# A recurrent layer's block pipeline: projections in another order, scores by pairs of heads, short products inside units, one staged transposition

## The chip, the cores and the metric

The kernel runs on one core of a Trainium2 chip. The number that counts is the device time of one execution in microseconds (us). The core's engines work side by side, each through its own list of instructions in the order of that list: TensorE (PE; its weight loads are shown as PEld), VectorE (DVE), ScalarE (ACT), GpSimd (POOL) and SyncE (SP), which issues the DMA transfers. An instruction that waits for another engine holds up all that stand behind it in its list. Sums of products build up in PSUM, everything else lies in SBUF, in 128 partitions.

## The reference

For 4096 tokens of width 1024: a normalised and modulated input `h`, one input projection, two branches, one output projection, a residual and a final norm. The part that the change touches is the second branch, RWKV-7 with 8 heads of 64 values:

```python
r, w_lo, k, v, a_lo, z = jnp.split(seg, split_idx, axis=-1)    # after a shift by one token
w_raw = -jax.nn.softplus(-(w0 + jnp.tanh(w_lo) @ w_up)) - 0.5
decay = jnp.exp(-jnp.exp(w_raw))
a  = jax.nn.sigmoid(a0 + a_lo @ a_up)
kk = k * k_k / jnp.maximum(norm(k * k_k), L2_EPS)               # per head
k  = k * (1.0 + (a - 1.0) * k_a)
# per token and head, S is 64 x 64:
S = S * w_t + (S @ -kk_t)[..., None] * (kk_t * a_t) + v_t[..., None] * k_t
y = S @ r_t
y = (group_norm(y) * ln_w + ln_b + sum(r * k * r_k) * v) * silu(z)
```

## The kernel before

Phase 1 (to 397 us) makes `h` and the pooling branch. Phase 2 takes the tokens in 16 blocks of 256, each of 4 chunks of 64. The tail (from 1820 us) is the output projection. The change lies in phase 2.

Inside a chunk the recurrence is written with matrices. For each block the kernel goes through these stages:

- `front` (L525 to L646): 17 projections of the block's tokens, called segs: `lo` (0), and for each of four pairs of heads `p` keys `kS` (1+4p), receptances `rS` (2+4p), values `vS` (3+4p) and gates `zS` (4+4p). A seg is 8 units of three 128x257 matmuls in half precision (L552 to L554); then ScalarE (L556) and VectorE (L557) evict it. After `rS` of a pair follow its short products and the decay: `pl`, `pa` (L583, L584), `tw`, `ta` (L586 to L589), a scan `L` on VectorE (L591), its exponentials `Ppad`, `Pi` (L593, L595), and the scaled operands `AR` and `BK` (L605 to L609), `rk` (L614). `cent` (L621) makes the centred values `vps` of a pair and copies them into `UV`, for the last pair also the squared norms of the keys; `late` (L635) makes the bonus `bon`.
- `scores` (L648): for each chunk eight heads' products `BK` x `AR` on TensorE, masked by VectorE into `sc` (L666).
- `inverse` (L690): the 32 diagonal 32x32 blocks of each half are transposed by VectorE into `Ab` (L703), scaled (L704) and copied (L705, L707). Then 30 pairs of VectorE steps (`Wt` L721, `W` L726) eliminate them, each pair needing the one before. The results go back through transpositions (L739, L740) to the products `qp` (L750) and `m21p` (L758) of TensorE.
- `chain` (L789): the loop over the four chunks with the state `S`. In each: `px` (L809), copies `xa` on ScalarE (L816), `psn` (L821), copies `UV` on ScalarE (L829), `psn` and `px` again (L837, L848), copies `y` (L855). After every second chunk `gn` normalises: `ysq`, `var`, `rstd` on POOL (L870), `y` (L872), and then `ytp`, `mx` (L884 to L888).

While block b goes through `scores`, `inverse` and `chain`, the units of `front` of block b+1 are put between its products by `fill(n)`: n units each, the counts in `FS` to `FY` and `FI`. `unpin` and `keep_in_program_order` fix the order of some matmuls; beyond that the framework's scheduler orders each engine's list by priority, where `high_priority(offset=PRI)` lifts the elimination, `xa` and `UV` over the next block's front. PSUM tiles come from small pools: three buffers for `pj`, which segs, `pl`, `pa`, `vps` and `pb` share, two each for `sc` and `px`, one for `psn`. A buffer is free for TensorE only when its eviction is over.

Of the kernel before, what the change touches and what calls it, by code (L numbers as in the profile page):

```python
# [52 lines left out]
def kernel(  # L53
# [426 lines left out]
    with ExitStack() as ph:  # L480
# [56 lines left out]
        def front(b, f):  # L537
# [8 lines left out]

            def seg(m, name, bufs=2):
                pp = ps_pj.tile([P, TB2 + 1], F32, tag="pj", name=f"pj{b}_{m}")
                for k in range(KT):
                    if k:  # L550
                        yield
                    unpin(PE.matmul(pp, w2_hi[m][:, k, :], hh[k], start=(k == 0), stop=False))  # L552
                    PE.matmul(pp, w2_hi[m][:, k, :], hl[k], start=False, stop=False)  # L553
                    PE.matmul(pp, w2_lo[m][:, k, :], hh[k], start=False, stop=(k == KT - 1))  # L554
                sg = wk.tile([P, TB2], F32, tag=name, name=f"{name}{b}_{m}", bufs=bufs)
                A.activation(sg, pp[:, 1:], AF.Identity, bias=0.0, scale=c1[:, m : m + 1])  # L556
                V.scalar_tensor_tensor(sg, pp[:, :TB2], c2[:, m : m + 1], sg, op0=ALU.mult, op1=ALU.add)  # L557
                return sg
# [12 lines left out]
            todo = []  # L571
            sqs = []
            for p in range(NPAIR):
                kS = yield from seg(1 + 4 * p, "kS")
                sq = wk.tile([P, TB2], F32, tag=f"sq{p}", name=f"sq{b}_{p}")
                sqs.append(sq)
                A.activation(sq, kS, AF.Square, scale=vec[:, V_KK + p : V_KK + p + 1])
                yield
                rS = yield from seg(2 + 4 * p, "rS")
# [16 lines left out]
                if todo:  # L596
                    todo.pop(0)()
                yield
                vS = yield from seg(3 + 4 * p, "vS")
                if p == 0:  # L600
                    BK = f["BK"] = blk.tile([P, NPAIR, NCH, 2, C], F32, tag="BK", name=f"BK{b}")
# [5 lines left out]
                V.tensor_mul(ta, ta, kS)  # L607
                V.tensor_mul(AR[:, p, :, 1, :], c3(rS), Pp[:, :, 1:])
                V.tensor_mul(BK[:, p, :, 1, :], c3(ta), c3(Pi))  # L609
                G.tensor_copy(pc[:, p, :], Pp[:, :, C])  # L610
                if todo:
                    todo.pop(0)()
                rk = wk.tile([P, TB2], F32, tag="rk", name=f"rk{b}_{p}")
                V.scalar_tensor_tensor(rk, rS, pv[:, HRK, p : p + 1], ta, op0=ALU.mult, op1=ALU.mult)  # L614
                yield
                zS = yield from seg(4 + 4 * p, "zS")
                tz = wk.tile([P, TB2], F32, tag="L", name=f"tz{b}_{p}")
                A.activation(tz, zS, AF.Tanh, bias=0.0, scale=0.5)
                V.scalar_tensor_tensor(szt[:, p, :], tz, 1.0, zS, op0=ALU.add, op1=ALU.mult)

                def cent(p=p, vS=vS):  # L621
                    vps = ps_pj.tile([P, 4, P], F32, tag="pj", name=f"vps{b}_{p}")
                    for j in range(2):
                        PE.matmul(vps[:, j, :], vS[:, j * P : (j + 1) * P], cmat, start=True, stop=True)
                    if p == NPAIR - 1:
                        for q in range(NPAIR):
                            PE.matmul(vps[32 * q : 32 * q + 32, 2:4, :], hsel, sqs[q].rearrange("q (j t) -> q j t", j=2), start=True, stop=True)
                        A.copy(ssb.rearrange("q (j t) -> q j t", j=2), vps[:, 2:4, :])
                    for j in range(2):
                        A.copy(  # L630
                            UV[64:128].rearrange("q (c j) e -> q c j e", j=2)[:, :, j, p * P : (p + 1) * P],
                            vps[64 * j : 64 * j + 64, 0:2],
                        )

                def late(p=p, rk=rk, vS=vS):  # L635
                    pb = ps_pj.tile([P, TB2], F32, tag="pj", name=f"pb{b}_{p}")
                    PE.matmul(pb, bones, rk, start=True, stop=True)
                    V.tensor_mul(bon[:, p, :], pb, vS)  # L638

                todo = [cent, late]  # L640
                if p < NPAIR - 1:
                    yield
            f["todo"] = todo
            yield

        def scores(b, f, fill):  # L646
# [271 lines left out]
        def project(b):  # L918
# [128 lines left out]
```

## Time and profile before

| | |
|---|---|
| median of 3 runs | 2123.24 us (2123.21 to 2123.97) |
| the profiled execution | 2123.65 us, span 2121.9 us |
| mean granted clock of TensorE | 0.982 of full speed |
| PE busy | 1984.5 us (94%) |
| DVE busy | 1449.5 us (68%) |
| ACT busy | 965.5 us (46%) |
| POOL busy | 131.6 us (6%) |

Busy shares are means over phases with different limits: phase 1 and the tail are near full on TensorE alone. Matmuls overlap, so that one of them shows 0.27 us while the next begins 0.11 us later; the distance of starts is the price then. An operation on DVE or ACT overlaps its neighbour by somewhat under 0.1 us.

### The profile page before, as it was taken

To read this page: it belongs to the slowest core of one execution; us is meant where nothing else is said; L and a number is where in the kernel's file an instruction comes from. 1 tells how busy PE (TensorE), PEld (TensorE's weight loads), DVE (VectorE), ACT (ScalarE), POOL (GpSimd) and SP (SyncE) were. 2 spreads that over 40 slices of the span, in tenths; PEclk is the share of its full clock that TensorE was granted. 3 is DMA by queue.
4 is the path that set the end of the run, shared out by engine and by line. 5 is a ranking of instruction groups with operands and counts; after the bars stand their busy time and mean duration, and the time that the engine had idled before them with its cause. 6 is when DMAs were issued, how large, how long until landed. Compare 5 with 4: busy or idle time off the path is not lost.

```text
span 2121.9 us, 48336 instructions
## 1 busy us (share of the span) xinstructions
PE 1984.5 (94%) x20186; PEld 1463.6 (69%) x20186; DVE 1449.5 (68%) x3549; ACT 965.5 (46%) x2119; POOL 131.6 (6%) x262
## 2 busy tenths in 40 slices
PE   5999999999999999999999999999999989999998
PEld 2444444677777777777777777777777767788886
DVE  7898987566857768578577686786776866533333
ACT  3545433345455554554555545545555453312111
POOL 0000000000000000000000100000000000100000
PEclk8999999999999999999999999999999999999999
DMA  8867767200110110101101101011011434443431
GB/s 304 278 224 239 243 217 269 66 21 2 31 27 7 31 26 7 32 2 31 27 7 31 27 6 32 2 31 27 6 32 27 134 111 140 157 142 130 153 105 70
DMA packets 140445, 183.19 MB, mean 86 GB/s; under 512 B 12098, under 2 KB 94018, under 8 KB 140227
## 3 DMA queue, kind: packets, MB, share of 16 engines
q1 hardware_dynamic: 140226, 180.11, 26.0%
q8 instruction: 158, 2.59, 0.5%
q14 instruction: 61, 0.49, 0.1%
HBM read 121.22 MB, written 58.85 MB: 85 GB/s over the span
## 4 chain that ended last, share of the span: by engine, by line
PE 54%; DVE 28%; ACT 11%; issue 4%; DMA 2%; POOL 0%; SPq 0%; DVEq 0%; ACTq 0%; POOLq 0%
PE po L947 6%; PE po L949 5%; PE po L948 5%; PE pj L552 5%; PE pj L554 4%; PE pj L553 4%; DVE W L726 4%; DVE Wt L721 4%; PE pp L412 4%; PE pp L411 4%; PE pp L410 4%; DVE Ab L703 3%; PE psn L821 2%; PE scp_sc L659 2%; PE px L809 2%
## 5 line engine op out<-in xcount | busy, mean ns | idle before, releaser
L552 PE MATMUL pj<-hh,w2h 128*128 128x257 f16 x2176 | 609.5, 280 | 48.2 <-DVE bon L638 24.0
L554 PE MATMUL pj<-hh,w2l 128*128 128x257 f16 x2176 | 604.1, 278 | 0.0
L553 PE MATMUL pj<-hl,w2h 128*128 128x257 f16 x2176 | 602.3, 277 | 0.0
L553 PEld LDWEIGHTS <-w2h 128*128 128x128 f16 x2176 | 217.5, 100 | 87.4 <-issue 57.4
L552 PEld LDWEIGHTS <-w2h 128*128 128x128 f16 x2176 | 214.9, 99 | 52.2 <-issue 6.5
L554 PEld LDWEIGHTS <-w2l 128*128 128x128 f16 x2176 | 213.5, 98 | 34.1
L947 PE MATMUL po<-wo,mh 128*128 128x512 f32 x512 | 204.3, 399 | 3.7 <-ACT mh L931 3.7
L948 PE MATMUL po<-wo,mh 128*128 128x512 f32 x512 | 201.8, 394 | 0.0
L411 PE MATMUL pp<-lo,w1h 128*128 128x512 f16 x512 | 194.0, 379 | 1.4 <-DVE lo L225 1.4
L410 PE MATMUL pp<-hi,w1h 128*128 128x512 f16 x512 | 194.1, 380 | 1.1 <-ACT hi L224 1.1
L412 PE MATMUL pp<-hi,w1l 128*128 128x512 f16 x512 | 194.0, 379 | 0.0
L951 DVE TENSOR_TENSOR x<-po,x 128x512 f32<-128x512 f32 x64 | 44.2, 690 | 151.9 <-PE po L949 151.9
L953 ACT ACTIVATE sq<-x 128x512 f32<-128x512 f32 x64 | 40.4, 631 | 208.8 <-DVE x L951 190.6
L721 DVE TENSOR_TENSOR Wt<-W,Ab 128x30 f32<-128x30 f32 (+7 forms) x480 | 117.5, 245 | 10.2
L726 DVE TENSOR_TENSOR W<-W,Wt 128x30 f32<-128x30 f32 (+7 forms) x480 | 117.5, 245 | 9.1
L947 PEld LDWEIGHTS po<-wo,mh 128*128 128x128 f32 x512 | 96.7, 189 | 25.9 <-ACT mh L931 3.9
L948 PEld LDWEIGHTS po<-wo,mh 128*128 128x128 f32 x512 | 96.6, 189 | 22.3
L949 PE MATMUL po<-wo,ml 128*128 128x512 f32 x256 | 101.4, 397 | 0.0
L557 DVE SCALAR_TENSOR_TENSOR kS<-pj,c,kS 128x256 f32<-128x256 f32 x64 | 30.6, 478 | 100.2 <-ACT kS L556 100.2
L412 PEld LDWEIGHTS <-w1l 128*128 128x128 f16 x512 | 50.1, 98 | 61.6 <-issue 2.0
L411 PEld LDWEIGHTS <-w1h 128*128 128x128 f16 x512 | 50.1, 98 | 59.4 <-issue 1.2
L410 PEld LDWEIGHTS <-w1h 128*128 128x128 f16 x512 | 50.2, 98 | 59.0 <-issue 0.8
(243 smaller groups left out, 3814.0 us busy)
## 6 DMA issues: line engine op xcount, KB each, us to landing
x<-in_x_dram SPq DMA_DIRECT2D x64, 256.0 KB, 3.0
out_dram<-x SPq DMA_DIRECT2D x64, 256.0 KB, 2.1
xk<-in_xT_dram SPq DMA_DIRECT2D x56, 256.0 KB, 4.1
xt<-in_x_dram SPq DMA_DIRECT2D x28, 512.0 KB, 5.7
wada<-in_w_ada_dram SPq DMA_DIRECT2D x24, 512.0 KB, 5.7
w2raw<-in_w_in_dram SPq DMA_DIRECT2D x17, 512.0 KB, 5.4
hh<-hT_hi SPq DMA_DIRECT2D x32, 257.0 KB, 3.6
hl<-hT_lo SPq DMA_DIRECT2D x32, 257.0 KB, 3.0
```

Source lines behind the costliest of these rows:

```text
L410: PE.matmul(pp, w1_hi[m][:, k, :], hi, start=(k == 0), stop=False)
L411: PE.matmul(pp, w1_hi[m][:, k, :], lo, start=False, stop=False)
L412: PE.matmul(pp, w1_lo[m][:, k, :], hi, start=False, stop=(k == KT - 1))
L552: unpin(PE.matmul(pp, w2_hi[m][:, k, :], hh[k], start=(k == 0), stop=False))
L553: PE.matmul(pp, w2_hi[m][:, k, :], hl[k], start=False, stop=False)
L554: PE.matmul(pp, w2_lo[m][:, k, :], hh[k], start=False, stop=(k == KT - 1))
L703: V.transpose(Ab[o : o + 32], sc[o : o + 32, :, o : o + 32].rearrange("s i t -> s t i"))
L721: V.tensor_mul(tmp[:, :n, :k], W[:, r0:, k : k + 1].to_broadcast([P, n, k]), Ab[:, k : k + 1, :k].to_broadcast([P, n, k]),)
L726: V.tensor_add(W[:, r0:, :k], W[:, r0:, :k], tmp[:, :n, :k])
L947: unpin(PE.matmul(po, mh[:, k, ts_], wo[0][k][n], start=(k == 0), stop=False))
L948: PE.matmul(po, mh[:, k, ts_], wo[1][k][n], start=False, stop=False)
L949: PE.matmul(po, (ml[:, k] if b % 2 == 0 else ml[k])[:, ts_], wo[0][k][n], start=False, stop=(k == KT - 1))
```

## The change

Five edits in `front`, `scores` and `inverse`. The segs come in another order: `lo`, the four `zS`, the four `vS`, and then `kS` and `rS` of each pair. The short products wait in a list `pend` and are issued inside a later seg, ahead of its units 3 and 6, in place of between segs. They are `cent` (now two products only), `heavy` (the decay and the operands of a pair) and `bonus`. The keys' norms become a function of their own, `norms`, whose products have 256 columns and a PSUM tile of their own. `scores` goes by pairs of heads, all four chunks at a time, in place of by chunks with all heads. After each pair's masks ScalarE copies the diagonal blocks into the free half of `UV` (`stg`), in the order that lets `inverse` use one transposition of 64 partitions in place of two of 32. `vS` gets four buffers, `tz` its own tag.

```diff
+            pend = []
             def seg(m, name, bufs=2):
...
+                    if k in (3, 6) and pend:
+                        pend.pop(0)()
...
             for p in range(NPAIR):
-                kS = yield from seg(1 + 4 * p, "kS")
...
+                zS = yield from seg(4 + 4 * p, "zS")
+                tz = wk.tile([P, TB2], F32, tag="tz", name=f"tz{b}_{p}")
+                A.activation(tz, zS, AF.Tanh, bias=0.0, scale=0.5)
+                V.scalar_tensor_tensor(szt[:, p, :], tz, 1.0, zS, op0=ALU.add, op1=ALU.mult)
                 yield
-                rS = yield from seg(2 + 4 * p, "rS")
+
+            def cent(p, vS):
+                vps = ps_pj.tile([P, 2, P], F32, tag="pj", name=f"vps{b}_{p}")
+                for j in range(2):
+                    PE.matmul(vps[:, j, :], vS[:, j * P : (j + 1) * P], cmat, start=True, stop=True)
...
+            for p in range(NPAIR):
+                vS = yield from seg(3 + 4 * p, "vS", bufs=NPAIR)
+                vs.append(vS)
+                pend.append(lambda p=p, vS=vS: cent(p, vS))
+                yield
...
+            def heavy(p, kS, rS):
...
+            def bonus(p):
+                pb = ps_pj.tile([P, TB2], F32, tag="pj", name=f"pb{b}_{p}")
+                PE.matmul(pb, bones, rks[p], start=True, stop=True)
+                V.tensor_mul(bon[:, p, :], pb, vs[p])
...
+            def norms():
+                pn = ps_pj.tile([P, TB2], F32, tag="pj", name=f"pn{b}")
+                for q in range(NPAIR):
+                    PE.matmul(pn[32 * q : 32 * q + 32, :], hsel, sqs[q], start=True, stop=True)
+                A.copy(ssb, pn)
+
+            for p in range(NPAIR):
+                kS = yield from seg(1 + 4 * p, "kS")
...
+                if p:
+                    pend.append(lambda p=p - 1: bonus(p))
                 yield
...
+                rS = yield from seg(2 + 4 * p, "rS")
+                pend.append(lambda p=p, kS=kS, rS=rS: heavy(p, kS, rS))
                 if p < NPAIR - 1:
                     yield
-            f["todo"] = todo
+            while pend:
+                pend.pop(0)()
+            f["todo"] = [norms, lambda: bonus(NPAIR - 1)]
...
-            for ch in range(NCH):
...
+            stg = f["stg"] = f["UV"][0:64].rearrange("q c e -> q (c e)")[:, 0:1024].rearrange("q (t i) -> q t i", t=32)
+            for p in range(NPAIR):
...
+                for kb in range(2):
+                    o = 32 * kb
+                    A.copy(
+                        stg[o : o + 32].rearrange("q t (c g h) -> q t c g h", c=NCH, h=2)[:, :, :, p],
+                        sc[o : o + 32, :, o : o + 32].rearrange("q (c g h) t -> q t c g h", c=NCH, h=2)[:, :, :, p],
                     )
...
-                for kb in range(2):
-                    o = 32 * kb
-                    V.transpose(Ab[o : o + 32], sc[o : o + 32, :, o : o + 32].rearrange("s i t -> s t i"))
+                V.transpose(Ab[0:64], f["stg"])
```

Three places show how the lists move. In the names, the number behind a seg is its own (`vS_3` is the values of pair 0), `_0` to `_3` behind the others is the pair or the chunk, and `Wt_30` is the first elimination step; line numbers of the changed kernel are its own. The first place is VectorE between the last masks and the first step. Before:

```order
L666 TENSOR_TENSOR sc_12765<-scp_3_px,mask 128x4x128
L557 SCALAR_TENSOR_TENSOR kS_1_12915<-pj_1_12844,c_103,kS_1_12915 128x256
L703 STREAM_TRANSPOSE Ab_12936<-sc_12765 32x1024 x2
L638 TENSOR_TENSOR bon_11578<-pb_3_12927,vS_15_12654 128x256
L704 TENSOR_TENSOR Ab_12936<-Ab_12936,d2T_12764 64x1024
L557 SCALAR_TENSOR_TENSOR rS_2_12956<-pj_2_12920,c_103,rS_2_12956 128x256
L707 COPY W_12937<-Ab_12936 64x512 x2
L591 SCALAR_TENSOR_TENSOR L_0_12968<-rst,tw_0_12963 128x256
L721 TENSOR_TENSOR Wt_30_13037<-W_12937,Ab_12936 128x30
L726 TENSOR_TENSOR W_12937<-W_12937,Wt_30_13037 128x30
```
Now:

```order
L687 TENSOR_TENSOR sc_12826<-scp_3_sc,mask 128x4x128
L687 TENSOR_TENSOR sc_12826<-scp_3_px,mask 128x4x128
L562 SCALAR_TENSOR_TENSOR zS_4_12983<-pj_4_12921,c_103,zS_4_12983 128x256
L728 STREAM_TRANSPOSE Ab_13002<-UV_11636 64x1024
L582 SCALAR_TENSOR_TENSOR szt_12852<-tz_0_12986,zS_4_12983 128x256
L729 TENSOR_TENSOR Ab_13002<-Ab_13002,d2T_12825 64x1024
L562 SCALAR_TENSOR_TENSOR zS_8_13021<-pj_8_12989,c_103,zS_8_13021 128x256
L732 COPY W_13003<-Ab_13002 64x512 x2
L746 TENSOR_TENSOR Wt_30_13082<-W_13003,Ab_13002 128x30
L751 TENSOR_TENSOR W_13003<-W_13003,Wt_30_13082 128x30
```
One transposition stands in place of two; `bon`, `rS_2` and the scan `L_0` have left the stretch, and `zS_4`, `zS_8` and a product `szt` of the gates stand there.

The second place is VectorE where the values of pair 0 are evicted (L557 before, L562 now), on which `vps` of TensorE waits. Before, inside the fourth pair of steps:

```order
L726 TENSOR_TENSOR W_12937<-W_12937,Wt_28_13056 128x2x28
L608 TENSOR_TENSOR AR_12787<-rS_2_12956,Ppad_3664 128x4x64
L721 TENSOR_TENSOR Wt_27_13077<-W_12937,Ab_12936 128x2x27
L557 SCALAR_TENSOR_TENSOR vS_3_13022<-pj_3_12979,c_103,vS_3_13022 128x256
L726 TENSOR_TENSOR W_12937<-W_12937,Wt_27_13077 128x2x27
L607 TENSOR_TENSOR ta_0_12965<-ta_0_12965,kS_1_12915 128x256
```
Now, between the 14th pair and the 15th:

```order
L751 TENSOR_TENSOR W_13003<-W_13003,Wt_18_13210 128x7x18
L746 TENSOR_TENSOR Wt_17_13231<-W_13003,Ab_13002 128x7x17
L751 TENSOR_TENSOR W_13003<-W_13003,Wt_17_13231 128x7x17
L562 SCALAR_TENSOR_TENSOR vS_3_13159<-pj_3_13128,c_103,vS_3_13159 128x256
L746 TENSOR_TENSOR Wt_16_13234<-W_13003,Ab_13002 128x8x16
L751 TENSOR_TENSOR W_13003<-W_13003,Wt_16_13234 128x8x16
```
The eviction of `vS_3` has moved behind the step `Wt_17`, and the front's products around it are gone.

The third place is ScalarE in the third chunk (chunk 2) of the chunk loop. Before:

```order
L855 COPY y_0_13567<-px_0_13469 64x4x64
L855 COPY y_0_13567<-px_1_13470 64x4x64
L865 ACTIVATE ysq_0_13755<-y_0_13567 128x512
L604 ACTIVATE ta_3_13720<-ta_3_13720,pv 128x256
L816 COPY xa_2_13787<-px_0_13469 64x256
L816 COPY xa_2_13787<-px_1_13470 64x256
L829 COPY UV_11581<-psn_2_13769 64x4x64 x2
L855 COPY y_2_13770<-px_0_13469 64x4x64
```
Now (`UV` from `psn_2` is the copy for which TensorE waits):

```order
L880 COPY y_0_13614<-px_1_13492 64x4x64
L890 ACTIVATE ysq_0_13786<-y_0_13614 128x512
L841 COPY xa_2_13818<-px_0_13491 64x256
L841 COPY xa_2_13818<-px_1_13492 64x256
L611 ACTIVATE tw_2_13828<-pl_2_13824,pv 128x256
L613 ACTIVATE ta_2_13830<-pa_2_13825,pv 128x256
L614 ACTIVATE tw_2_13828<-tw_2_13828,one 128x256
L618 ACTIVATE Ppad_3664<-L_2_13833 128x4x64
L620 ACTIVATE Pi_2_13836<-L_2_13833 128x256
L854 COPY UV_11636<-psn_2_13800 64x4x64 x2
L626 ACTIVATE ta_2_13830<-ta_2_13830,pv 128x256
```
The copies `UV` from `psn_2` came right behind `xa_2`; now `tw`, `ta`, `Ppad` and `Pi` of pair 2 stand between.

## Rows read from the trace of the kernel before

**Rows 1.** Windows of block 7: length, busy us of PE, PEld, DVE, ACT, POOL, clock, DMA, GB/s

```profile
1045.60:1068.60 23.00, 21.29 (x203) 16.98 (x202) 17.88 (x32) 10.89 (x24) 1.88 (x3) 1.00 0.19 50
1068.60:1092.90 24.30, 22.56 (x184) 18.57 (x181) 22.31 (x85) 9.90 (x23) 0.86 (x4) 0.93 0.01 1
1102.10:1130.40 28.30, 26.69 (x605) 20.56 (x602) 12.71 (x38) 18.34 (x48) 1.93 (x2) 1.00 0.07 19
1045.60:1130.40 84.80, 78.83 (x1062) 62.57 (x1060) 61.38 (x169) 45.02 (x107) 6.05 (x11) 0.98 0.08 20
```

**Rows 2.** Waits of PE in block 7: us in total, times, longest

```profile
PE pj L552 <- DVE bon L638: 1.7, 1, 1.7
PE vps L624 <- ACT tw L586: 1.7, 3, 0.6
PE pj L552 <- DVE rS L557: 1.2, 1, 1.2
```

**Rows 3.** Timeline of DVE, block 7, masks to elimination: start, us, instruction

```profile
1060.35 0.68 DVE L666 TENSOR_TENSOR sc<-scp_px,mask 128x512 f32<-128x512 f32 x1
1061.34 3.87 DVE L703 STREAM_TRANSPOSE Ab<-sc 32x1024 f32<-32x1024 f32 x2
1067.99 0.69 DVE L591 TENSOR_TENSOR_SCAN L<-rst,tw 128x256 f32<-128x256 f32 x1
1068.60 0.16 DVE L721 TENSOR_TENSOR Wt<-W,Ab 128x30 f32<-128x30 f32 x1
```

**Rows 4.** Groups by line, whole span: busy us, mean ns of one, idle before

```profile
L740 DVE STREAM_TRANSPOSE MQ<-UV 32x1024 f32<-32x1024 f32 x16 | 19.6, 1223 | 0.8 <-ACT sq L953 0.8
L752 ACT COPY MQ<-qp 32x256 f32<-32x256 f32 x64 | 23.3, 364 | 1.6
L721 DVE TENSOR_TENSOR Wt<-W,Ab 128x30 f32<-128x30 f32 (+7 forms) x480 | 117.5, 245 | 10.2
```

**Rows 5.** Timeline of PE, block 7, around vps; idle before in brackets

```profile
1078.64 0.71 PE L624 MATMUL vps<-cmat,vS 128*128 128x128 f32 x4 [0.57 <-ACT tw L586]
1080.52 0.37 PE L552 MATMUL pj<-hh,w2h 128*128 128x257 f16 x1 [1.17 <-DVE rS L557]
1080.91 0.42 PE L554 MATMUL pj<-hh,w2l 128*128 128x257 f16 x1
1081.12 0.42 PE L552 MATMUL pj<-hh,w2h 128*128 128x257 f16 x1
```

**Rows 6.** Timeline of PE, block 7, chunk 0

```profile
1109.14 0.27 PE L553 MATMUL pj<-hl,w2h 128*128 128x257 f16 x1
1109.25 0.27 PE L554 MATMUL pj<-hh,w2l 128*128 128x257 f16 x1
1109.65 0.69 PE L837 MATMUL psn<-UV,BT 128*64 128x64 f32 x16
```

**Rows 7.** Timeline of ACT, block 7, chunk loop

```profile
1105.72 1.51 ACT L760 COPY UV<-m21p 32x256 f32<-32x256 f32 x4 [0.80 <-PE m21p L758]
1108.86 0.75 ACT L829 COPY UV<-psn 64x256 f32<-64x256 f32 x2 [0.84 <-PE psn L821]
1115.85 0.47 ACT L586 ACTIVATE tw<-pl,pv 128x256 f32<-128x256 f32 x1 [0.15 <-PE pa L584]
1116.58 0.51 ACT L589 ACTIVATE tw<-tw,one 128x256 f32<-128x256 f32 x1
1117.89 0.42 ACT L593 ACTIVATE Ppad<-L 128x256 f32<-128x256 f32 x1
1118.22 0.40 ACT L595 ACTIVATE Pi<-L 128x256 f32<-128x256 f32 x1
```

**Rows 8.** Group of the power on POOL, whole span

```profile
L870 POOL TENSOR_TENSOR rstd<-var,nhalf 128x8 f32<-128x8 f32 x32 | 54.0, 1687 | 218.9 <-DVE var L868 218.9
```

**Rows 9.** Windows of the first front and of block 4

```profile
397.60:451.30 53.70, 52.08 (x450) 44.24 (x449) 27.39 (x61) 23.60 (x54) 0.75 (x4) 1.00 0.02 7
790.30:874.40 84.10, 77.57 (x1062) 61.93 (x1061) 61.40 (x168) 44.94 (x108) 6.06 (x11) 1.00 0.08 20
```

More of the change, by code (lines that the diff above doesn't have):

```diff
@@ L570, in front @@
             c3 = lambda t_: t_.rearrange("q (c t) -> q c t", c=NCH)
-            todo = []
-            sqs = []
             for p in range(NPAIR):
-                kS = yield from seg(1 + 4 * p, "kS")
-                sq = wk.tile([P, TB2], F32, tag=f"sq{p}", name=f"sq{b}_{p}")
-                sqs.append(sq)
-                A.activation(sq, kS, AF.Square, scale=vec[:, V_KK + p : V_KK + p + 1])
+                zS = yield from seg(4 + 4 * p, "zS")
+                tz = wk.tile([P, TB2], F32, tag="tz", name=f"tz{b}_{p}")
+                A.activation(tz, zS, AF.Tanh, bias=0.0, scale=0.5)
+                V.scalar_tensor_tensor(szt[:, p, :], tz, 1.0, zS, op0=ALU.add, op1=ALU.mult)
                 yield
-                rS = yield from seg(2 + 4 * p, "rS")
+            def cent(p, vS):
+                vps = ps_pj.tile([P, 2, P], F32, tag="pj", name=f"vps{b}_{p}")
+                for j in range(2):
+                    PE.matmul(vps[:, j, :], vS[:, j * P : (j + 1) * P], cmat, start=True, stop=True)
+                for j in range(2):
+                    A.copy(
+                        UV[64:128].rearrange("q (c j) e -> q c j e", j=2)[:, :, j, p * P : (p + 1) * P],
+                        vps[64 * j : 64 * j + 64],
+                    )
+            vs = []
+            for p in range(NPAIR):
[3 more added lines that the diff above has]
+                yield
+            rks = {}
+            def heavy(p, kS, rS):
                 ps_ = slice(p * P, (p + 1) * P)
@@ L595, in front @@
                 A.activation(Pi, L, AF.Exp, bias=0.0, scale=-cexp)
[L596 to L599, printed above, removed]
                 if p == 0:
-                    BK = f["BK"] = blk.tile([P, NPAIR, NCH, 2, C], F32, tag="BK", name=f"BK{b}")
+                    f["BK"] = blk.tile([P, NPAIR, NCH, 2, C], F32, tag="BK", name=f"BK{b}")
+                BK = f["BK"]
                 tb = wk.tile([P, TB2], F32, tag="L", name=f"tb{b}_{p}")
@@ L614, in front @@
                 V.scalar_tensor_tensor(rk, rS, pv[:, HRK, p : p + 1], ta, op0=ALU.mult, op1=ALU.mult)
-                yield
[L616 to L640, printed above, removed]
+            def bonus(p):
+                pb = ps_pj.tile([P, TB2], F32, tag="pj", name=f"pb{b}_{p}")
+                PE.matmul(pb, bones, rks[p], start=True, stop=True)
+                V.tensor_mul(bon[:, p, :], pb, vs[p])
@@ L652, in scores @@
             BT = blk.tile([P, NCH, 512], F32, tag="BT", name=f"BT{b}")
-            for ch in range(NCH):
-                pts = [pool.tile([P, 512], F32, tag=tg, name=f"scp{b}_{ch}_{tg}") for pool, tg in ((ps_sc, "sc"), (ps_x, "px"))]
-                for j in range(4):
+            stg = f["stg"] = f["UV"][0:64].rearrange("q c e -> q (c e)")[:, 0:1024].rearrange("q (t i) -> q t i", t=32)
+            for p in range(NPAIR):
+                pts = [pool.tile([P, 512], F32, tag=tg, name=f"scp{b}_{p}_{tg}") for pool, tg in ((ps_sc, "sc"), (ps_x, "px"))]
+                for j in range(NCH):
                     for hq in range(2):
@@ L666, in scores @@
                     V.tensor_mul(
-                        sc[:, ch * NH : (ch + 1) * NH, :].rearrange("q (j h) t -> q j h t", h=2)[:, :, hq],
-                        pts[hq].rearrange("q (j t) -> q j t", j=4),
-                        mask.unsqueeze(1).to_broadcast([P, 4, P]),
+                        sc.rearrange("q (c h) t -> q c h t", h=NH)[:, :, 2 * p + hq],
+                        pts[hq].rearrange("q (j t) -> q j t", j=NCH),
+                        mask.unsqueeze(1).to_broadcast([P, NCH, P]),
+                    )
+                for kb in range(2):
+                    o = 32 * kb
+                    A.copy(
+                        stg[o : o + 32].rearrange("q t (c g h) -> q t c g h", c=NCH, h=2)[:, :, :, p],
+                        sc[o : o + 32, :, o : o + 32].rearrange("q (c g h) t -> q t c g h", c=NCH, h=2)[:, :, :, p],
                     )
                 fill(FS + 1)
-                if ch == 2:
+                if p == 2:
                     pt = ps_sc.tile([P, 512], F32, tag="sc", name=f"d2p{b}")
@@ L682, in scores @@
                         V.transpose(d2T[64 * g : 64 * g + 64], d2)
-                if ch in (0, 3):
+                if p < 2:
                     f["todo"].pop(0)()
+                    run(gns[0], 1)
                 fill(FS)
-                if ch % 2 == 0:
-                    run(gns[0], 1)
             f["sc"], f["BT"], f["d2T"] = sc, BT, d2T
@@ L925, in project @@
                 mh = blk.tile([P, KT, TB2], F32R, tag="BK", name=f"mh{b}")
-                ml = [wk.tile([P, TB2], F32R, tag=n, name=f"ml{b}_{n}{i}", bufs=2) for i in range(2) for n in ("kS", "rS", "vS", "zS")]
+                ml = [
+                    wk.tile([P, TB2], F32R, tag=n, name=f"ml{b}_{n}{i}", bufs=m)
+                    for n, m in (("kS", 2), ("rS", 2), ("vS", NPAIR)) for i in range(m)
+                ]
             for q, src in enumerate((mixp_d, mixr_d)):
```

14 lines of the change are left out of this document (8 added, 6 removed).

## The prediction

> **What bounds the kernel now.** I read the header of the page first: 2123.65 us for the profiled execution, 2121.9 us of it span, 1.75 us around it. All sums below are made against 2123.65; the median of the runs, 2123.24, is 0.4 us less, and I take that off at the end. Then I cut one steady block out of the middle (block 7, 84.8 us; by their first score product blocks 1 to 14 all take 84.1 to 85.0) and had its stages shown one by one [rows 1]. The reader is to see three things there. TensorE is busy in 78.83 of 84.80 us, so at most about 6 us a block show as idle. VectorE is nearly full (22.31 of 24.30) in one stage alone, the elimination. ScalarE is nowhere full, but in the chunk loop it works 18.34 of 28.30 us. Third, the waits of TensorE in the block [rows 2]: it waits for VectorE's evictions and for ScalarE's `tw`, each 1 to 2 us a block. So neither engine alone is the bound: the block is a relay, in which scores, masks, transposition and elimination run on VectorE, while TensorE fills the time with the next block's projections and then waits for their evictions in VectorE's list. The third view, a timeline of VectorE from the last mask to the first step of the elimination [rows 3], gives the transposition's price: 3.87 us for two.
>
> I count from the block's start (1045.6). Four marks in before: last mask ends at 15.4 (1060.35 + 0.68), first elimination step 23.0, `qp` starts 56.5 (1102.1), first `psn<-UV,BT` 64.05 [rows 6], end 84.8.
>
> **Scores to the first elimination step: 21.1 for 23.0.** The first mask now stands on VectorE behind the products of the last pair (the rest of `heavy(3)`), and TensorE gets `pa`, `pn` and `pb` there in place of `vps`: I estimate 0.6, so the last mask ends at 16.0. From it to the first step before took 7.6. Removed: one transposition of 64x1024 in place of two of 32x1024. Nearest row with as many columns per partition: 1223 ns [rows 4], so 3.87 - 1.22 = 2.65 gone. Also gone from this stretch is the scan of `L` (0.69, of which 0.6 not overlapped [rows 3]). Added: the last pair's two staging copies between mask and transposition, and the wait for them. Other edits there (`szt`, `zS` in place of `kS`, `bon`, `rS`) are alike in number and shape. What a staging copy costs, the trace doesn't show: 32x256 out of SBUF, two neighbouring elements at 512 B. Low end: a ScalarE copy of as many elements, 364 ns [rows 4]. High end: that times 1927/1223, which is what the same source stride costs VectorE between its two transpositions (3.87/2 against 1.22), 0.575 us. I take the high end, since that row has the very stride; both ends stay in the range (0.2 us of a copy, eight of them a block on ScalarE and two on the path, are worth 0.7 us a block). With 0.575 two overlapped copies and their hand-over make 0.9 beyond the eviction that hides the rest. 7.6 - 2.65 - 0.6 + 0.9 = 5.2; 16.0 + 5.2 is about 21.1. The six earlier copies have the score units on TensorE as cover (VectorE 17.88 and ScalarE 10.89 of 23.0 [rows 1]); if that cover went, each would cost its 0.575.
>
> The two transpositions, 3.87 us against 1.22 for as many columns, tell what a stride of 512 B costs. [...]
>
> **Elimination: VectorE wins 7 us, TensorE 2.** 24.3 us is 60 steps of 0.245 [rows 4] with 0.034 between them (16.7), 25 front instructions in between at 0.27 each (6.75) and a wait of 0.8. The order now leaves 8 of the 25: 16.7 + 2.2 = 18.9, and VectorE is through at 40.0 for 47.3. But TensorE doesn't win that. Its next product `vps` of pair 0 needs `vS_3`, whose eviction stands behind the 28th step: 21.1 + 28 x 0.279 + 5 x 0.27 + 0.45 = 30.7. From there on TensorE has its own work: 52.7 units of three matmuls at 0.112 (pitch in [rows 6]) = 17.7; four `vps` of 0.45 = 1.8; `pl`, `pa` 0.55; `pb` and the leading `px` 1.35; switches between shapes 0.8; evictions not ready at once, `rk` for `pb` above all, 1.5. Sum 23.7, so `qp` starts at 54.4, before 56.5: **-2.1**. What is late next is thus no longer VectorE's chain, but TensorE's own list behind `vS_3`.
>
> **Chunk loop: +2.2.** `heavy(1..3)` now falls here, and ScalarE takes its list in order. After the four copies of `qp` stand `tw`, `ta`, `tw`, `Ppad`, `Pi` of pair 1 (0.47, 0.47, 0.51, 0.42, 0.40 [rows 7], less 0.1 overlap each: 1.9) and a wait for the scan of 0.3, and only then the copies of `m21p`, for which `xa`, `UV` and so TensorE's `psn` wait. Before, ScalarE idled 0.8 there for `m21p`. 1.9 + 0.3 - 0.8 = **1.4**; first `psn<-UV,BT` at 54.4 + 7.55 + 1.4 = 63.35. In chunk 2 the two `UV` copies of `psn_2` came right behind `xa` and `psn` (for chunk 0: [rows 7]); now `tw`, `ta`, `tw`, `Ppad`, `Pi` stand ahead. `Ppad` waits for the scan of pair 2, this stands on VectorE behind `y_0`, and that behind POOL's `rstd` (1687 ns [rows 8]). TensorE's idle time there comes out at 1.9; it replaces a `vps` (0.45) with its wait for `tw` (0.6 [rows 2]), which stood in that loop before: **+0.8**. 20.75 + 0.8 = 21.55, end at 84.9.
>
> Per block: -2.1 + 1.4 + 0.8 = +0.1. With the copies at their low end -0.6.
>
> **Edges.** The first front has no elimination to hide in: TensorE idles 1.6 of 53.70 us there [rows 9], for `tw` and `up`. In the new order short products stand inside units, so that goes, and block 0 wins 1.9 in its scores: -3.5. Block 15 has no next front, and the tail's loads wait for block 14's last rows, which the new order sends out later: 0 to 4.6, the middle 2.3. Both edges -1.2. Sum 2123.65 + 15 x 0.1 - 1.2 = 2123.9, less 0.4 for the median: **2123.5**.
>
> **Rivals.** (1) *Faster: the chunk loop hides its new work.* For it: ScalarE is free there for 10 of 28.3 us [rows 1], and the scheduler's list is only late where a wait of VectorE meets it; if scans come early, neither 1.4 nor 0.8 shows. Against: the order itself, `UV` behind `Ppad`. Time: 15 x -2.1 - 1.2 = 2091; with the half-speed stretches below gone as well, 0.8 in some 12 blocks, 2081.
> (2) *Slower: TensorE's clock falls in the chunk loop.* [...] Block 4, without such a stretch (mean 1.00), takes 84.1 [rows 9] for 84.8, so one costs 0.7 to 0.8 net; 12 of the 14 steady blocks have one. [...] It decides from the point at which both stay and each is followed by such a stretch: 2 x 0.8 a block, 15 x 1.7 - 1.2 = 2148. Against: in the chunk loop the matmuls around are short, and in before it runs at 1.00 with idle times up to 0.4.
>
> [...]
>
> **How the numbers follow.** Forecast 0.46, rival 1 0.29, rival 2 0.25. The forecast is a difference of two terms of 2 us a block, each good to some 0.6, so its own range is wide, 2106 to 2142 (low end: copies at 0.364 and half of the 0.8 gone; high end: 0.5 more wait in either loop and the upper bound of the tail). 0.2% is 4.2 us, about what a measurement of this kernel can tell from no change; of the forecast's 0.46, about 0.17 lies below that, 0.13 within and 0.16 above. Faster: 0.29 + 0.17 = 0.46; within 0.13; slower 0.25 + 0.16 = 0.41. The range takes in most of both rivals: 2084 to 2154.
>
> **What would show it.** Right: the first step of the elimination 2 us earlier in a steady block, one transposition of 1.2 us, elimination of about 19 us; `vps` of pair 0 starts directly behind the eviction of `vS_3`; `qp` about 2 us earlier; ScalarE's `UV<-psn` of chunk 2 some 2 us later behind its `psn`; stage copies between 0.36 and 0.58. Wrong would be: copies over 0.6 us, or `vps` not waiting; a chunk loop of 28.3 us or less (rival 1); a granted clock below 1 between `qp` and the block's end (rival 2).

## The result, and the profile after

The changed kernel takes 2172.02 us (2171.55 to 2172.84, 4 runs) for 2123.22: 1.023 times as long, 95% interval 1.0212 to 1.0248. That is 48.8 us more, above the stated range of 2084 to 2154. The profiled execution took 2172.32 us.

I again count from a block's start. For blocks 1 to 14 the marks of the two traces are, as medians (in brackets the smallest, which is that of blocks without a half-clock stretch in that part, a stretch in which TensorE's granted clock is half of full speed, as in block 7 before, 0.50 from 1080.6 to 1083.9 us):

| us after the block's start | before | after | predicted |
|---|---|---|---|
| last mask ends | 15.5 | 16.2 | 16.0 |
| first elimination step | 23.0 | 21.5 | 21.1 |
| length of the elimination | 24.3 (23.5) | 19.7 (18.9) | 18.9 |
| `qp` starts | 56.5 (55.7) | 56.1 (55.2) | 54.4 |
| `qp` to first `psn<-UV,BT` | 7.55 | 8.65 (8.65) | 8.95 |
| chunks 1 to 2 / 2 to 3 | 6.2 / 6.2 | 8.1 / 7.9 (6.4) | |
| whole block, mean | 84.8 (84.1) | 87.7 (85.6) | 84.9 |

From `qp` to the first `psn<-UV,BT`, six of the 14 blocks after take 9.8 to 10.1 us, with a stretch there. No block after is free of stretches; its 85.6 adds up the smallest values of each part, 55.2 + 8.65 + 6.1 (chunks 0 to 1) + 8.1 + 6.4 + 1.1 (the last products).

The windows of two blocks after (block 8 by stage, block 8 whole, block 9 whole; columns as in [rows 1]):

```profile
1153.10:1174.60 21.50, 19.55 (x194) 15.69 (x192) 17.46 (x39) 14.11 (x30) 1.98 (x2) 1.00 0.20 53
1174.60:1193.50 18.90, 16.75 (x144) 14.25 (x145) 17.16 (x67) 7.17 (x17) 0.48 (x4) 1.00 0.01 2
1193.50:1208.40 14.90, 13.73 (x127) 10.98 (x125) 10.49 (x21) 7.49 (x16) 1.38 (x2) 1.00 0.01 3
1208.40:1240.20 31.80, 28.23 (x605) 20.87 (x604) 15.55 (x44) 20.79 (x54) 2.01 (x3) 0.95 0.07 18
1153.10:1240.20 87.10, 78.26 (x1062) 61.80 (x1060) 60.67 (x168) 49.56 (x116) 5.85 (x11) 0.98 0.08 20
1240.20:1329.50 89.30, 81.57 (x1065) 63.33 (x1062) 60.84 (x169) 49.75 (x116) 5.84 (x11) 0.94 0.07 19
```

The stretch from scores to the end of elimination is 6.9 us shorter than in [rows 1]; all of it and more is given back between there and the block's end. Blocks 8 and 9 do the same work, and differ in the clock column: 0.98 and 0.94. A block now takes 86.5 or 87.1 us with one half-clock stretch in it, 88.2 to 88.3 with two and 89.2 to 89.5 with three. From block 1's start to block 15's the granted clock shows 24 of them (8 in the elimination, 6 behind `qp`, 10 in chunk 3), before 12.

Waits of TensorE in block 8 after, which answer to [rows 2]:

```profile
PE psn L862 <- ACT UV L854: 2.2, 2, 1.7
PE btp L738 <- ACT BT L739: 1.9, 1, 1.9
PE vps L588 <- DVE vS L562: 1.5, 2, 1.2
PE psn L846 <- ACT xa L841: 1.1, 1, 1.1
PE pb L638 <- DVE rk L634: 0.8, 1, 0.8
PE d2p L703 <- ACT mx L911: 0.7, 1, 0.7
```

None of the three of before is left, and there are more new ones: their sum goes from 5 to 8 us. VectorE between the last mask and the first step in block 8 (answers to [rows 3]), and the group of the staging copies over the whole span:

```profile
1168.58 0.68 DVE L687 TENSOR_TENSOR sc<-scp_px,mask 128x512 f32<-128x512 f32 x1
1170.62 1.24 DVE L728 STREAM_TRANSPOSE Ab<-UV 64x1024 f32<-64x1024 f32 x1 [0.97 <-ACT UV L695]
1174.57 0.19 DVE L746 TENSOR_TENSOR Wt<-W,Ab 128x30 f32<-128x30 f32 x1
```

```profile
L695 ACT COPY UV<-sc 32x256 f32<-32x256 f32 x128 | 81.7, 639 | 76.3 <-DVE sc L687 75.3
```

The transposition is as priced, 1.24 us in one. A copy takes 0.64 us, above my high end of 0.575. The third place that the change's section shows, ScalarE in chunk 2 of block 8, now runs like this:

```profile
1225.87 0.76 ACT L841 COPY xa<-px 64x256 f32<-64x256 f32 x2
1227.66 0.51 ACT L614 ACTIVATE tw<-tw,one 128x256 f32<-128x256 f32 x1
1229.81 0.42 ACT L618 ACTIVATE Ppad<-L 128x256 f32<-128x256 f32 x1 [1.65 <-DVE L L616]
1230.14 0.40 ACT L620 ACTIVATE Pi<-L 128x256 f32<-128x256 f32 x1
1230.44 0.73 ACT L854 COPY UV<-psn 64x256 f32<-64x256 f32 x2
```

`Ppad` holds ScalarE for 1.65 us, and `UV` from `psn_2`, which needs nothing of `Ppad`, stands behind it. What TensorE does meanwhile, and after:

```profile
1229.17 0.33 PE L909 MATMUL ytp<-ident,y 128*128 128x128 f32 x1
1231.22 0.69 PE L862 MATMUL psn<-UV,BT 128*64 128x64 f32 x16 [1.72 <-ACT UV L854]
1232.86 0.42 PE L557 MATMUL pj<-hh,w2h 128*128 128x257 f16 x1
1233.08 0.42 PE L558 MATMUL pj<-hl,w2h 128*128 128x257 f16 x1
1233.29 0.42 PE L559 MATMUL pj<-hh,w2l 128*128 128x257 f16 x1
```

TensorE is idle for 1.72 us, and the next projections start 0.21 us apart in place of 0.11, as in [rows 5]: the granted clock is 0.50 of full speed from 1232.5 to 1235.9 us. In blocks where this follows, chunk 3 takes 7.9 us, in the others 6.4, with the same instructions.

### The profile page after: what moved, and what is told of

The parts are those of the page before. It is cut to its first block, busy times and chain, and to the rows that moved or that the text cites. A ratio compares the mean times of both kernels' runs of the same rounds, so it can differ in the third digit from the quotient of the medians.

```text
span 2170.6 us, 48415 instructions
## 1 busy us (share of the span) xinstructions
PE 2000.9 (92%) x20186; PEld 1462.9 (67%) x20186; DVE 1435.8 (66%) x3533; ACT 1039.2 (48%) x2247; POOL 127.7 (6%) x262
## 4 chain that ended last, share of the span: by engine, by line
PE 56%; DVE 24%; ACT 12%; issue 3%; DMA 2%; POOL 1%; SPq 0%; ACTq 0%; DVEq 0%; POOLq 0%
PE po L975 5%; PE po L977 5%; PE po L976 5%; PE pj L557 5%; DVE W L751 4%; PE pj L559 4%; PE pj L558 4%; DVE Wt L746 4%; PE pp L411 4%; PE pp L412 4%; PE pp L410 4%; PE scp_sc L680 2%; DVE sc L687 2%; PE pb L638 2%; DVE L L616 2%
## 5 line engine op out<-in xcount | busy, mean ns | idle before, releaser
L557 PE MATMUL pj<-hh,w2h 128*128 128x257 f16 x2176 | 613.0, 282 | 0.8 <-ACT up L425 0.8
L557 PEld LDWEIGHTS <-w2h 128*128 128x128 f16 x2176 | 215.6, 99 | 68.8 <-issue 24.0
L695 ACT COPY UV<-sc 32x256 f32<-32x256 f32 x128 | 81.7, 639 | 76.3 <-DVE sc L687 75.3
L616 DVE TENSOR_TENSOR_SCAN L<-rst,tw 128x256 f32<-128x256 f32 x64 | 43.9, 687 | 100.2 <-ACT tw L614 100.2
L977 PE MATMUL po<-wo,ml 128*128 128x512 f32 x256 | 101.7, 398 | 0.0
L590 ACT COPY UV<-vps 64x256 f32<-64x256 f32 x128 | 46.8, 366 | 107.3 <-PE vps L588 106.5
```

The source lines that it names most:

```text
L616: V.tensor_tensor_scan(L, rst, tw, 0.0, op0=ALU.mult, op1=ALU.add)
L977: PE.matmul(po, (ml[:, k] if b % 2 == 0 else ml[k])[:, ts_], wo[0][k][n], start=False, stop=(k == KT - 1))
```

## The experiments

Full speed and clock can be told apart inside a trace where blocks with and without stretches stand side by side. The table has the ratio to the kernel before with its interval, and from the profiled execution a block's mean, the shortest block, the half-clock stretches that begin between block 1's start and block 15's, and the length of block 15.

| kernel | us | ratio | mean / shortest block | stretches | block 15 |
|---|---|---|---|---|---|
| before | 2123.2 | 1 | 84.8 / 84.1 | 12 | 94.6 |
| changed | 2172.0 | 1.023 (1.0212 to 1.0248) | 87.7 / 86.5 | 24 | 101.7 |
| 1 scores half alone | 2147.6 | 1.0112 (1.0097 to 1.0127) | 86.7 / 85.9 | 15 | 95.4 |
| 2 front half alone | 2181.9 | 1.0275 (1.0259 to 1.0291) | 88.6 / 86.1 | 26 | 95.7 |
| 3 no power | 2131.8 | 1.0034 (1.0024 to 1.0043) | 85.4 / 84.8 | 5 | 99.1 |
| 4 idle times filled | 2235.1 | 1.0531 (1.0514 to 1.0549) | 92.1 / 91.5 | 22 | 99.7 |
| 5 unit 6 | 2146.7 | 1.011 (1.0093 to 1.0127) | 86.3 / 85.5 | 18 | 99.8 |
| 6 values first | 2135.4 | 1.0057 (1.0042 to 1.0072) | 85.3 / 85.0 | 4 | 100.1 |
| 7 = 5 and 6 | 2134.1 | 1.0051 (1.0036 to 1.0066) | 85.3 / 84.8 | 9 | 99.8 |
| 8 values first, unit 7 | 2117.7 | 0.9977 (0.9966 to 0.9988) | 84.2 / 84.2 | 0 | 97.7 |
| 9 = 8, bonus later | 2094.5 | 0.9865 (0.9851 to 0.9878) | 83.0 / 82.9 | 0 | 93.8 |
| 10 = 8, no staging | 2126.6 | 1.0015 (1.0004 to 1.0025) | 84.9 / 83.9 | 11 | 97.8 |
| 11 = 9, unit 5 | 2132.2 | 1.0041 (1.0029 to 1.0054) | 85.5 / 85.3 | 15 | 99.8 |
| 12 = 9, no staging | 2094.3 | 0.9862 (0.9844 to 0.9881) | 83.0 / 82.7 | 4 | 94.5 |

Executions of one kernel differ in the same way, with the same instructions. The ten of kernel 8 go from 2113.7 us at a mean granted clock of 0.993 to 2123.7 us at 0.987, the ten of kernel 3 from 2127.5 at 0.989 to 2135.1 at 0.985. It is not so everywhere: the five of kernel 11 take 2131.0 to 2132.2 us, at 0.979 as at 0.988.

**1 and 2: which half.** The first takes `scores` and the transposition of the changed kernel with the front of before (and one line that holds the first `qp` in its place); the second the reverse. The change has one more edit, which its section does not name: in `scores`, the next step of `gn` and the two products left over from the front (`todo`) now stand behind pairs 0 and 1, where they stood behind chunks 0 and 2, and 0 and 3. Kernel 2 has this edit, kernel 1 has not; nothing was run to price it.

```diff
-  PE.matmul(pt[...], sc[0:32, i, 32:64], MQ[0:32, i, :], start=True, stop=True)      # qp, in 1
+  ordered(PE.matmul(pt[...], sc[0:32, i, 32:64], MQ[0:32, i, :], start=True, stop=True, ...))
```

> The kernel before with the second half of the change alone: scores by pairs of heads, staging copies on ScalarE, one transposition; front (order of projections, short products) as before. The first product of qp is held behind the projections ahead of it, as it stood before. Theory A (the loss sits in the front's new order: short products that fall into the chunk loop, and the half-clock stretches behind the new idle times): first elimination step at 21.0 to 21.5 us after the block's start, elimination still about 24 us with 25 front instructions in it, chunk loop as before, so 1 to 2 us a block less: 2095 to 2110 us. Theory B (the loss sits in the staging copies, which take 0.64 us each on ScalarE in place of 0.36): the loss stays, 2140 us or more.

> The changed kernel with the first half of the change alone: new order of the projections and short products inside units, but scores by chunks with all heads and two strided transpositions as before. Theory A: the chunk loop's 22 to 23 us from psn<-UV,BT to the end and the half-clock stretches stay, and the 1.5 us that the single transposition saved are lost again: 2180 to 2200 us. Theory B: without the copies the loss goes: 2115 to 2140 us.

Both halves lose alone. Only 2 was as expected; the time of 1 lies in theory B's range. In 1 the first step comes at 21.0 and the elimination ends 3.3 us sooner, with a chunk loop as before, and yet `qp` starts at 58.1 for 56.5. Against the extra line as the reason, TensorE runs as many matmuls of each kind ahead of `qp` as before, 318 of them projections. TensorE's longest waits in block 7 of kernel 1, and what stands on ScalarE ahead of the longest:

```profile
PE vps L624 <- ACT tw L586: 4.3, 3, 3.2
```

```profile
1098.81 1.04 ACT L747 COPY UV<-UV 32x1024 f32<-32x1024 f32 x1 [1.48 <-DVE UV L745]
1099.87 0.47 ACT L556 ACTIVATE rS<-pj,c 128x256 f32<-128x256 f32 x1
1100.25 0.47 ACT L586 ACTIVATE tw<-pl,pv 128x256 f32<-128x256 f32 x1
1100.77 1.23 PE L624 MATMUL vps<-cmat,vS 128*128 128x128 f32 x4 [3.23 <-ACT tw L586]
```

With the sooner chain, ScalarE's copy of `UV` behind the elimination, which waits for VectorE's closing transpositions, stands ahead of the eviction `rS` of pair 2 and of its `tw`. `tw` is what `vps` waits for, and TensorE idles 3.2 us. So theory A's prize of the scores half fell, for the reason that the prediction gave for the elimination: VectorE wins, TensorE doesn't. The copies' price (theory B) can't be all of the loss either: kernel 2 has none, and loses more. There `vps` waits up to 3.6 us for `vS`.

**3: the wait in chunk 2.** In `gn`:

```diff
-            G.tensor_tensor(rstd, var, nhalf[:, :NH], op=ALU.pow)
+            V.tensor_copy(rstd, var)
```

> The changed kernel, with the power -1/2 of the group norm left out (POOL's 1.7 us; VectorE copies the variance in its place, so the output is not the reference's). Theory A (in chunk 2 UV<-psn_2 waits behind Ppad, this for the scan, this behind y_0 on VectorE, this for POOL): the distance of psn<-UV,BT of chunks 1 and 2 falls from 8.08 to 6.2 to 6.6 us, the idle time of 1.7 us of TensorE there goes, and with it the half-clock stretch in chunk 3 (10 of 14 blocks, 1.5 us each): 2130 to 2150 us. Rival (ScalarE's own work in the loop, 19 us, is the bound, not the wait): 2160 us or more.

TensorE's list is that of the changed kernel, instruction by instruction. The time is 40 us less, as expected. ScalarE and a whole block of kernel 3:

```profile
1210.47 0.42 ACT L618 ACTIVATE Ppad<-L 128x256 f32<-128x256 f32 x1 [0.82 <-DVE L L616]
1211.09 0.73 ACT L854 COPY UV<-psn 64x256 f32<-64x256 f32 x2
```

```profile
1219.40:1304.20 84.80, 76.57 (x1062) 60.89 (x1060) 60.91 (x170) 49.42 (x116) 2.43 (x9) 1.00 0.08 20
```

The wait is 0.8 us shorter, chunks 1 and 2 are 7.25 apart in place of 8.08 (6.2 to 6.6 expected), and no chunk 3 has a stretch any more. That alone would be 14 x 0.8 = 11 us and the stretches there. But those behind `btp` in the elimination went too, though that idle time of 1.9 us is still there: 5 stretches are left of 24, all behind `qp`, and the clock is the larger part of the 40 us (11 us from the wait, some 22 from stretches).

**4: the idle times filled.**

```diff
+                if ch == 3 and b + 1 < NB2:
+                    idle_work(ps_s.tile([P, 512], F32, tag="psn", name=f"iw{b}"), 16)
...
+                if ch == 2 and b + 1 < NB2:
+                    idle_work(psn, 15)      # matmuls of 256 columns that nobody reads
```

> The changed kernel with matmuls that nobody needs, 16 ahead of the last btp of a block and 15 ahead of psn<-UV,BT of chunk 2, in a PSUM tile that is free there: they take up the two idle times of TensorE of 1.7 to 1.9 us, and nothing else changes. [...]

I expected 2140 to 2158 us if each half-clock stretch follows from such an idle time, and 2168 or more if the clock falls for another reason or its fall costs nothing. It took 2235.1, 77 us above the first range, and doesn't test the clock, since new waits arose. Two of TensorE's waits in its block 8:

```profile
PE vps L588 <- DVE vS L562: 4.1, 2, 3.3
PE psn L803 <- ACT UV L860: 1.7, 1, 1.7
```

L803 are the added matmuls: they wait 1.7 us for the copies `UV` themselves, though they write the half of the tile that those copies don't read. The ones ahead of `btp` took up the idle time there, but in this kernel `vS_3` stands later among the elimination's steps, and a wait of 3.3 us arose.

**5, 6 and 7: two causes moved out of the way.**

```diff
-                    if k in (3, 6) and pend:
+                    if k == 6 and pend:                   # 5 and 7
...
-            for p in range(NPAIR):                        # 6 and 7: the loop over zS
-                zS = yield from seg(4 + 4 * p, "zS")      # stands behind that over vS
```

> The changed kernel with one number changed: the short products are issued ahead of unit 6 of a seg alone, in place of units 3 and 6. heavy(2) of the chunk loop then stands behind the copies UV<-psn_2 on ScalarE, heavy(1) behind those of m21p, and pb behind the first qp. Theory A (the chunk loop loses by the copies that stand behind heavy on ScalarE, and by the half-clock stretches that follow the idle times): psn<-UV,BT of chunks 1 and 2 6.2 to 6.5 us apart (8.08 with the change), qp earlier by 0.5 to 1 us, no half-clock stretch in chunk 3 (10 of 14 blocks have one with the change): 2100 to 2130 us. Rival (the loop is filled by the work itself, wherever it stands): 2155 us or more.

> The changed kernel with the values' projections ahead of the gates' (vS, then zS). vS_3 and vS_7 are then evicted before the elimination begins, and the first vps has nothing to wait for in it. Theory A (TensorE's list behind vS_3 sets the time of qp): the wait of vps for vS_3 (1.4 us, plus three of 0.4 to 0.6) goes, qp 1.5 to 2.5 us earlier after the block's start (55.2 with the change), the chunk loop as with the change: 2135 to 2155 us. Rival (the wait only moves to another eviction, since VectorE's list of 60 steps is the bound): qp at 55 us, 2165 us or more.

> Both together: values ahead of the gates, and short products ahead of unit 6 alone. By theory A the two gains add: 2065 to 2100 us, faster than the kernel before. By the rival (what is gained in one place is waited for in the next): no less than the better one of the two alone.

5 does what it should in chunk 2 (5.85 us), but `heavy(3)` falls into the next block's first scores, where `pb` waits 2.7 us for `rk` (last mask at 18.7 for 16.2). A second `pb` stands between the first `qp` products and waits 0.7 us, so that `qp` to the first `psn<-UV,BT` takes 10.1 us. 25 us of the loss go, not 42 or more. 6 fell within its range by another road: `qp` is 0.6 us earlier at full speed, not 1.5 to 2.5, as the wait moves on to later pairs. Waits and window of its block 9:

```profile
PE vps L581 <- DVE vS L562: 2.3, 3, 1.2
PE psn L862 <- ACT UV L854: 2.2, 2, 1.7
```

```profile
1217.10:1302.10 85.00, 77.07 (x1064) 61.12 (x1060) 60.64 (x169) 49.69 (x116) 5.86 (x11) 1.00 0.08 20
```

The idle time of 1.7 us in chunk 2 is untouched, that at `btp` is gone, and 4 stretches are left. So in 6 as in 3, where one of the two idle times is shorter, the stretches behind both went. 7 shows no sum of gains: it is as fast as 6 within their scatter, and the rival holds for it.

**8 and 9: waits one by one.** In 8 the number is 7. In 9 each entry of `pend` has its own unit, 7 for all but the bonus, which comes a seg later:

```diff
-                if p:
-                    pend.append(lambda p=p - 1: bonus(p))      # behind kS
...
+                if p:
+                    pend.append((3, lambda p=p - 1: bonus(p))) # behind rS
+                pend.append(((7, 7, 7, 7)[p], lambda p=p, kS=kS, rS=rS: heavy(p, kS, rS)))
```

> As the one before, but short products ahead of unit 7: heavy(1) also stands behind UV<-psn_0 on ScalarE; in turn xa_3 stands behind Ppad of heavy(2), and the first two score products of the next block stand early in TensorE's list, between other products. Theory A: qp to the first psn<-UV,BT 7.6 us as before the change (8.7 with it), chunk 3 longer by up to 1 us; 2060 to 2110 us.

> The kernel with values first and short products ahead of unit 7, in which pb of pair 0 cut into qp and waited 1.05 us for rk on VectorE: the bonus of each pair is now issued one seg later, ahead of unit 3 of the next pair's keys. Theory A (what TensorE waits for in the list is what the block takes, wait by wait): the wait for rk goes, qp to the first psn<-UV,BT 8.4 to 8.9 us (9.65 with unit 7 alone), the rest as there, no half-clock stretch: 2098 to 2110 us. Rival (the wait returns behind the next eviction): 2114 us or more.

8 is the first kernel faster than before, by 0.2% and short of the range expected; 9 is faster by 1.35%, a little more than expected. In both no stretch is left in blocks 1 to 14. Block 8 of kernel 9 (whole, then its three longest waits of TensorE):

```profile
1113.80:1196.70 82.90, 78.21 (x1064) 62.03 (x1060) 60.88 (x169) 49.20 (x115) 5.83 (x11) 1.00 0.08 21
```

```profile
PE btp L738 <- ACT BT L739: 0.8, 1, 0.8
PE px L834 <- ACT y L880: 0.7, 1, 0.7
PE vps L581 <- DVE vS L562: 0.7, 2, 0.4
```

TensorE is busy 78.2 us, as in block 8 after; what is gone is idle time. For 8 the 7.6 us from `qp` that I expected came out at 9.65, in part by the `pb` that then waited 0.9 us inside `qp`; 9 took that away and got 8.2.

**10, 11 and 12: staging, and unit 5.** 10 and 12 leave the `A.copy` of the staging out and transpose twice as before the change; 11 puts `heavy(0)` and `heavy(2)` ahead of unit 5.

> The kernel with values first and unit 7, scores by pairs, but without the staging copies: two strided transpositions on VectorE as before the change. It prices staging where TensorE's waits are out of the way. Theory A (staging is worth the difference of the transpositions less its copies, 1.1 us a block, and the last block gets back some 3 us): 2125 to 2137 us against 2117.65. Rival (TensorE's list, not the elimination's start, sets the block): 2114 to 2121 us.

> As the one before, but heavy(0) and heavy(2) ahead of unit 5 in place of 7: heavy(2) then stands on ScalarE right behind UV<-psn_2 and ahead of y_2, and the score products of the next block keep their place behind it. Theory A: chunk 3, 8.8 us with unit 7 since xa_3 stood behind Ppad, falls to 6.5 to 7.5 us, but part of that was work moved from the next block's start; 2090 to 2108 us. Rival (idle times at the copies y return and with them the half-clock stretches): 2112 us or more.

> The fastest version so far (values first, unit 7, bonus a seg later; 2094.47 us) without the staging copies, with two strided transpositions. Theory A on the clock (an idle time of TensorE of 1.7 us or more is followed by a half-clock stretch in part of the blocks): a block without such a stretch takes 82.6 to 82.9 us (82.92 with staging), but the idle time at the last btp grows from 0.8 to 1.9 us, and stretches come in about half of the blocks: 2098 to 2110 us. Rival (staging itself is worth the 1.1 us that the elimination starts earlier in the changed kernel): every block 84 us, no stretches, 2107 to 2113 us. Were the idle time at btp without effect, 2088 to 2094 us.

Theory A had staging wrong. 12 is as fast as 9, and blocks without a stretch are shorter without staging: 82.7 for 82.9, and 83.9 for 84.2 in 10. The saved transposition is real, but the copies stand on ScalarE ahead of `ta` of `heavy(3)`, and the last mask ends at 17.2 with them and at 15.3 to 15.5 without. That 10 lies in theory A's range is the clock's doing. What the copies do change is the clock: without them `btp` waits 1.9 us for 0.8, and stretches return behind it in 6 blocks of kernel 10 (5 more stand behind `qp`) and in 4 of kernel 12. The two kinds of blocks of kernel 12 stand below; a stretch costs 0.5 us there, so that it comes out under the 2098 to 2110 us expected.

```profile
1112.10:1194.90 82.80, 77.35 (x1063) 62.18 (x1062) 63.41 (x169) 44.18 (x107) 5.84 (x11) 1.00 0.08 21
1277.60:1360.90 83.30, 78.66 (x1062) 63.09 (x1060) 63.52 (x169) 44.41 (x107) 5.83 (x11) 0.98 0.08 21
```

11 missed, and its rival holds: chunk 3 falls to 6.9 us, but `pb` waits 2.7 us at the block's start again, with a stretch there in every block of the profiled execution. Since its executions at a higher clock take as long, the waits and not the stretches are the loss there.

## Why the prediction was wrong

The waits were mostly the ones forecast; the sum over them was not, and the clock was left out of it. The 48.7 us between the two profiled executions are 14 x 2.92 = 40.9 in blocks 1 to 14, 7.1 in block 15 and 0.6 ahead of block 1.

- **The step that failed is the per-block sum of +0.1.** It set 84.9, a sum of TensorE's work at full speed and its waits, against 84.8 of block 7, which has a half-clock stretch in it. Like against like was 84.1, the row of block 4 in [rows 9], which I used only for the price of a stretch. So at full speed the forecast was itself +0.8 a block, and its +0.1 takes the stretches of before as gone (-0.7) without a reason. Measured is +1.5 at full speed (85.6 for 84.1).
- **The clock, +1.4 a block where the sum had -0.7.** Stretches cost 2.1 us a block (87.7 less 85.6), before 0.7 (84.8 less 84.1). I had new idle times in the sum and let none of them touch the clock; rival 2 did, with a stretch behind each of its two in the chunk loop (1.4 and 1.9 us), and got 0.25. Its place and its price for the chunk loop (1.6 a block) came out, but not as it has them: 16 stretches there cost 1.1 to 1.5 each, where it has two a block at 0.8, and those behind `qp` follow a wait of 0.8 us of `pb` for `rk` that it doesn't name. The other 0.5 a block stands behind `btp` in the elimination, which neither the sum nor a rival has. That the stretches hang on TensorE's waits and not on its work is shown best by 3, with 5 of them for the same list of TensorE; 6 and 9 have 4 and 0 with as many matmuls in another order.
- **Scores to elimination:** 21.5 for 21.1. The last mask was 0.2 late, a copy took 0.64 us for 0.575, and the terms as stated add up to 21.2.
- **Elimination:** 18.9 as worked out. `vps` of pair 0 starts at 31.2 for 30.7, right behind `vS_3`. From there to `qp` 24.1 for 23.7, so that at full speed `qp` wins 0.5 (55.2 for 55.7), where 54.4 would have won 1.3.
- **Chunk loop:** `qp` to `psn<-UV,BT` 8.65 for 8.95, from there to the end 21.7 for 21.55. The wait behind POOL is shown by 3.
- **Edges:** Before block 1 nothing was gained (-3.5 forecast, +0.6): inside units short products wait as well, four `pb` for `rk` 2.9 us in all. Block 15 lost 7.1 for 2.3, and not in the tail's loads, where the forecast had it, but in the scores:

```profile
1724.20:1742.90 18.70, 14.26 (x116) 10.98 (x115) 16.88 (x30) 9.93 (x19) 1.64 (x1) 0.91 0.48 149
1765.70:1792.20 26.50, 22.56 (x121) 17.45 (x118) 18.44 (x37) 15.38 (x29) 2.22 (x4) 0.62 0.39 118
```

These are block 15's scores up to the first elimination step, before and after. TensorE is busy 8.3 us longer with about as many matmuls: its granted clock is 0.50 for 20.5 us on end (1771.8 to 1792.3 us), from 6.1 us after the block's start, where `pb` has waited 2.0 us for `rk` between score products. The kernels of the table with such a stretch of 10 us or more there have a block 15 of 97.7 to 101.7 us, those with at most 3.4 us 93.8 to 95.7, and either half alone is among these. Later the last staging copies stand behind `BT` on ScalarE, and VectorE idles 3.0 us for them ahead of its transposition. How clock, wait and copies share the 7 us wasn't tried.

```profile
1771.77 1.16 PE L638 MATMUL pb<-rk,bones 128*128 128x256 f32 x2 [2.01 <-DVE rk L634]
```

```profile
1786.36 1.24 DVE L728 STREAM_TRANSPOSE Ab<-UV 64x1024 f32<-64x1024 f32 x1 [3.02 <-ACT UV L695]
```

Kernel 9 comes near rival 1's 2091 us, but by another sum: its `qp` starts at 52.9 and its chunk loop takes 30.0 us, where rival 1 has 54.4 and 28.3. What it does show is that the change with its values first and its short products issued elsewhere is faster than the kernel before.

Open: which of several idle times in a block is followed by a half-clock stretch. An idle time of 1.7 to 1.9 us stays without one in kernels 3 and 6, and has one in most blocks of the changed kernel; one of 0.8 us ahead of `qp` has one in 6 of its 14 blocks, and 0.7 to 0.9 us has none in kernel 8.

## What to carry to other kernels

Before a sum of durations is set against a measured stage, look whether that stage ran at full clock, and take a twin of it that did. Where engines take their lists in order, a burst of short work that itself has to wait (here five ScalarE operations of a pair, of which one waits for a scan) belongs behind the copy that the busiest engine waits for: chunks 1 and 2 lie 8.1 us apart with it ahead, 5.85 behind. But it may then hold up something else; kernels 7, 8 and 9, which differ only in where short products are issued, take 2134, 2118 and 2094 us. A chain made shorter on one engine shows in the total only if what stands around it in the other engines' lists moves forward as well: kernel 1's elimination ends 3.3 us sooner, and it loses 24 us.

## What was not expected of the hardware

- A ScalarE copy of 32x256 out of SBUF, whose elements lie 512 B or more apart, took 639 ns (L695 after), 1.75 times one out of PSUM (364 ns, L752 before). A copy of 32x1024 from SBUF to SBUF without that stride took 1045 ns (L741 before), so four times the elements cost 1.6 times as much. VectorE's transposition of 32x1024 took 1927 ns with that stride in its source (L703 before) and 1223 without it (L740 before), 1.58 times; that of 64x1024 out of the staged copy took 1236 (L728 after).
- Half-clock stretches followed, or began in, idle times of TensorE of 0.7 to 3.6 us in blocks 1 to 14. They lasted 3.4 us in most cases (3.41 each of the 24 after), and 10 to 20 us in block 15 of nine kernels (20.48 after). In the changed kernel one costs 0.9 us in the elimination, 1.1 to 1.4 behind `qp` and 1.5 in chunk 3; why not the same was not tested.
